# One bank for the modulation rows of eight column groups, and a new layout and order at the beginning of attention

## The chip, the cores and the metric

One core of one Trainium2 chip runs the whole program. Times are microseconds (us) on the device, from one launch to its end. A kernel is judged by the median of several runs; the profile comes from one execution and gives every instruction on the engines PE (TensorE), DVE (VectorE), ACT (ScalarE), POOL (GpSimd) and SP (SyncE, which here only issues transfers).

## The reference, cut to what matters

Two layers work on 1024 latent rows and 256 context rows of width 1024. Each begins with an adaLN modulation, whose rows come from a condition `c` for the latents and `c_ctx` for the context. Layer 0 is the attention layer and layer 1 the state-space (SSD) layer; the change lies in layer 0 and in the modulation of both.

```python
mod = silu(cond) @ w_ada[i] + b_ada[i]        # cond: c or c_ctx; 1024 x 3072 per layer
shift, scale, gate = split(mod, 3)
u = rms_normalize(h) * (1 + scale) + shift
q, k, v, g = split(u @ w_in)                  # 16 query heads of 64, 4 key/value heads
q, k = axial_rope(q), axial_rope(k)           # latents only
# latents, block of 128 queries: three neighbouring key blocks inside a band, and the 256 context keys
# context: its 256 queries see the 256 context keys
p = softmax(concat(q @ k.T / 8 (masked), sink))[..., :-1]
y = ((p @ v) * silu(g)) @ w_out
h = h + gate * y
```

## The kernel before

All matmuls of float32 data are done as three products of split operands (high and low part, `mm3`: lines L227, L228, L229), so each projection of 128 columns against 512 tokens is 24 matmuls, and against the 256 context tokens 24 shorter ones. Token groups are numbered 0 (first 512 latents), 1 (the other 512) and 2 (the context).

The kernel is written in a framework that keeps a priority per instruction (its place in the program, unless `high_priority(offset)` shifts it), orders each engine's queue from these and from the dependencies, and puts in the waits. Queues are then in order: an instruction that waits holds all behind it on its engine. `tc.issue_after(ins)` adds only an order, on the engine of `ins`. Pools are stacked in memory in the order in which they are opened; a tile of a new pool waits for those old tiles whose bytes it takes over, so what a tile lies on decides when it can first be written.

**Projection phase** (`qkvg`). After keys and values come eight column tiles of queries (`q_step`, weights `wq`) for groups 2 and 0, then eight of gates (`g_step`, `wg`) for group 2, the last four for group 0 too. A query tile passes through rope (L501 to L504 on DVE and POOL), is split (L522, L523 or L525, L526) and goes to DRAM in four transfers (L534, L535); a gate tile takes a tanh on ACT (L541), one DVE operation (L542) and one transfer (L543). Between them `fill` runs two or three steps of the list `ada`, the modulation of eight groups of 512 columns: (layer 0, n = 4, 5) and (layer 1, n = 0 to 5). A group has nine steps in `adaln_col`: eight loads of 256 KB (L181, buffers of the tags `wh` and `wl` in the pool `wv`); after every fourth load four matmuls (L185), each in its own 32 rows of the bank `aps`; and `fin`: ACT copies the bank (L189), and `modulation` turns the row with four small matmuls against `sel` (L201, two output columns), which also adds up the four row groups, and DVE adds the bias (L203). This turning is done eight times here and four times in the first phase (`ada0`).

**Attention** (`attention`). A unit is one key/value head `j` with one block `b` of 128 queries. `att_front` loads queries (`qs`, `qz` on POOL's queue, L614 and L620) and gates (`sgt`, L616), and for four heads does two-part scores into the bank pair `S` (L636 for latent keys, L637 for context keys), a masked reduction on DVE (L640) and an exponential on ACT (L642). `att_back` transposes the weights per key block (`pt`, L661), splits them (L665 on ACT, L666 on DVE), multiplies by the values (`pv`, L667 and L668), and ends with a normalisation (L674 to L684). The front runs one unit ahead (`AHEAD`). Units come in the order context (8 units of 2 key blocks), group 0 (16 units), group 1 (16 units). After each key block `tick` advances filler work in parts of three matmuls (`PARTS` = 8 for a projection): during context units the first `QC` = 5 items of the list `pr`, during group 0 the other eleven, during group 1 the output projections. `pr` holds the eight query tiles and then the eight gate tiles of group 1. A filler item first loads its weights (L220 on SP's queue), splits them (L213 on ACT, L215 on POOL), and has one bank, `pj`, for its sum.

**What lies on what.** The projection phase's pools are `wv` (17 KB a partition, with `cs32`), `wq` (30 KB: raw weights `wr`, split weights `wh`, `wl`) and `qp` (`cos`, `sin`, `qf`, `qh`, `ql`, ...). Attention's are `att` (41.5 KB, first `qz`, `qs`, then the rest), `wo` (the filler's `wr`, `wh`, `wl`) and `qp1` (`cos`, `sin`, ...). By these sizes `qz` and `qs` lie on `wv`, which the modulation uses to its end; the filler's `wr` lies on `wl` of the last gate tile, and the new `cos` on `qf`, which the last gate tile's transfer reads. In PSUM the first tile of `psT` is `S`, four banks that were `pt` and two of the four `pj`.

Of the kernel before, what the change touches and what calls it, by code (L numbers as in the profile page):

```python
# [9 lines left out]
F32 = mybir.dt.float32  # L10
# [42 lines left out]
QC = 5  # L53
TAILP = (3, 7)
# [49 lines left out]
class Kernel:  # L104
# [52 lines left out]
    def load_cond(self, p):  # L157
# [9 lines left out]
        self.sel = t(cp, [P, 2], F32, "sel")  # L167
        nc.vector.tensor_reduce(self.sel, self.ident.rearrange("p (j r) -> p r j", r=32)[:, 0:2], axis=mybir.AxisListType.X, op=ALU.add)
# [3 lines left out]
    def adaln_col(self, layer, n, pool, ps):  # L172

        nc, t = self.nc, self.t
        st = {}

        def step(k):
            if k == 0:
                st["ps"] = t(ps, [P, 512], F32, "aps", 2)
            raw = t(pool, [P, 4, P], F32, ("wh", "wl")[k // 4])  # L180
            nc.sync.dma_start(raw, self.a["w_ada"][layer, n, k].rearrange("p (a c) -> p a c", a=4))  # L181
            st[k] = raw
            if k % 4 == 3:
                for j in range(4):
                    nc.tensor.matmul(st["ps"][32 * j : 32 * j + 32], self.cs[:, k - 3 + j, :], st[k - 3 + j].rearrange("p a c -> p (a c)"), start=k == 3, stop=k == KT - 1)  # L185

        def fin():
            row = t(self.pq, [P, 512], F32, "qf")
            nc.scalar.copy(row, st["ps"])  # L189
            m = self.modulation(layer, n, row, ps)  # L190
            if n // 2 == 2 and layer == 0:
                nc.vector.tensor_scalar_mul(m, m, 0.5)

        return [lambda k=k: step(k) for k in range(KT)] + [fin]

    def modulation(self, layer, n, row, ps):
# [3 lines left out]
        for j in range(4):  # L200
            self.last_mod = nc.tensor.matmul(mt[:, 2 * j : 2 * j + 2], row[:, j * P : (j + 1) * P], self.sel, start=True, stop=True)  # L201
# [41 lines left out]
    def proj_g(self, out, pspool, ws, rH, rL, i, tag="pj", m=P, parts=1):  # L243
# [3 lines left out]
        ps = self.t(pspool, [P, 1024 if tag == "S" else 512], F32, tag)  # L247
# [50 lines left out]
    def layer0(self):  # L298
# [62 lines left out]
    def ada0(self, n, raw, ps):  # L361
# [3 lines left out]
        for k in range(KT):  # L365
            j = k % 4
            mm = nc.tensor.matmul(pj[32 * j : 32 * j + 32], self.cs[:, k, :], raw[k // 2][:, k % 2], start=k < 4, stop=k >= 4)
# [145 lines left out]
    def qk(self, p, pj, i, l=None):  # L513
        nc, t = self.nc, self.t
        n = TT[i][1]
        f = t(p, [P, 512], F32, "qf") if i < 2 else None
# [20 lines left out]
    def g_out(self, p, pj, x, i, tag="qf"):  # L537
        nc, t = self.nc, self.t
        n = TT[i][1]
        th = t(p, [P, 512], F32, tag)[:, :n]  # L540
# [10 lines left out]
    def qkvg(self, p, wk, wv, wvp):  # L551
# [35 lines left out]
        ada = []  # L587
        for layer, n in [(0, 4), (0, 5)] + [(1, n) for n in range(6)]:
            ada += self.adaln_col(layer, n, wvp, ps)
# [19 lines left out]
    def att_front(self, p, x, i, j, b):  # L609
        nc, t = self.nc, self.t  # L610
        ps = self.psA
        o = b * P - TT[i][0]
        qs = t(p, [P, R, P], F32R, "qs")
        nc.gpsimd.dma_start(qs, self.q_d[j][i][:, :, :, o : o + P].rearrange("e s d n -> (s d) e n"))  # L614
        sg = t(p, [P, 2, P], F32, "sgt")
# [13 lines left out]
        nm = t(p, [P, R], F32, "nm")  # L629
        sums = t(p, [P, R], F32, "sums")  # L630
        sms = []
        for r in range(R):
            S = t(ps, [P, 1024], F32, "S")
            for x, (qq, kk) in enumerate(((qs[:, r, :], self.kHH[j]), (qz[:, r, :], self.kL[j // 2]))):
                if k1 > k0:
                    nc.tensor.matmul(S[:, c0_:512], qq, kk[:, k0 * P : k1 * P], start=x == 0, stop=x == 1)  # L636
                nc.tensor.matmul(S[:, 512:768], qq, kk[:, LAT : LAT + CTX], start=x == 0, stop=x == 1)  # L637
            Sv = S[:, c0_:768]
            sm = t(p, [P, 640], F32, "sm")
# [8 lines left out]
        rs = t(p, [P, 2, 2, HD], F32, "rs", 2)  # L648
# [4 lines left out]
    def att_back(self, p, st, oH, oL, tick):  # L653
# [4 lines left out]
        for x, bb in enumerate(kb):  # L658
# [3 lines left out]
            ph = t(p, [P, R * P], F32R, "ph")  # L662
            pl = t(p, [P, R * P], F32R, "pl")
# [12 lines left out]
        co = t(p, [HD, 512], F32, "co")  # L676
        nc.scalar.copy(co, pv[HD:, :])
        ot = t(p, [P, 2, P], F32, "ot")
# [951 lines left out]
```

## Time and profile before

| | |
|---|---|
| Time, median of 3 runs | 1852.27 us (1848.69 to 1852.5) |
| The profiled execution | 1852.09 us, of which span 1850.4 us |
| PE busy | 1764.7 us, 95% of the span |
| DVE, ACT, POOL busy | 1171.9, 894.8, 803.8 us |
| Mean granted TensorE clock | 0.988 |
| Moved by DMA | 227.64 MB, 123 GB/s on average |

Busy time is a sum over an engine's instructions; where a wait ends, the view names the instruction that ended it. The queries and gates of the projection phase run from about 130 to 274 us, context units from 274 to about 345 us, the units of group 0 to about 526 us, and those of group 1 to about 720 us. The chain that ended last runs through PE for nearly all of the span.

### The profile page before, as it was taken

To read this page: it belongs to the slowest core of one execution; us is meant where nothing else is said; L and a number is where in the kernel's file an instruction comes from. 1 tells how busy PE (TensorE), PEld (TensorE's weight loads), DVE (VectorE), ACT (ScalarE), POOL (GpSimd) and SP (SyncE) were. 2 spreads that over 40 slices of the span, in tenths; PEclk is the share of its full clock that TensorE was granted. 3 is DMA by queue.
4 is the path that set the end of the run, shared out by engine and by line. 5 is a ranking of instruction groups with operands and counts; after the bars stand their busy time and mean duration, and the time that the engine had idled before them with its cause. 6 is when DMAs were issued, how large, how long until landed. Compare 5 with 4: busy or idle time off the path is not lost. (4 is left out here: it accounts for less than half of the span.)

```text
span 1850.4 us, 29176 instructions
## 1 busy us (share of the span) xinstructions
PE 1764.7 (95%) x10375; PEld 1506.2 (81%) x10375; DVE 1171.9 (63%) x2144; ACT 894.8 (48%) x1963; POOL 803.8 (43%) x1066
## 2 busy tenths in 40 slices
PE   6899998899999999989999999999999999999997
PEld 2697776788889687768889898988989898888886
DVE  4534426887777755684776757676675767766643
ACT  3812226677778765573443535344353534454422
POOL 2331107654456454202454554545455454554321
PEclk8999999999999999999999999999999999999998
DMA  8658856553355455321332333332232323455542
GB/s 313 233 135 254 250 160 150 132 124 88 95 129 131 105 147 169 127 67 43 83 74 78 81 77 78 80 89 69 77 93 65 86 72 99 150 170 166 177 137 69
DMA packets 212498, 227.64 MB, mean 123 GB/s; under 512 B 16384, under 2 KB 149632, under 8 KB 212352
## 3 DMA queue, kind: packets, MB, share of 16 engines
q1 hardware_dynamic: 178288, 207.12, 37.7%
q0 software_dynamic: 34064, 18.65, 5.6%
q8 instruction: 82, 1.34, 0.3%
q14 instruction: 64, 0.52, 0.1%
HBM read 190.88 MB, written 35.13 MB: 122 GB/s over the span
## 5 line engine op out<-in xcount | busy, mean ns | idle before, releaser
L227 PE MATMUL pj<-uH,wh 128*128 128x512 f32 (+1 forms) x712 | 257.7, 363 | 18.4 <-ACT uH L446 8.5
L228 PE MATMUL pj<-uL,wh 128*128 128x512 f32 (+1 forms) x712 | 244.9, 344 | 0.2 <-DVE uL L447 0.2
L229 PE MATMUL pj<-uH,wl 128*128 128x512 f32 (+1 forms) x712 | 244.2, 344 | 0.7 <-POOL wl L215 0.5
L1140 POOL TENSOR_TENSOR xw<-xn,dtdec 128x256 f32<-128x256 f32 x144 | 106.3, 741 | 197.2 <-PE psD L1165 125.0
L227 PEld LDWEIGHTS pj<-uH,wh 128*128 128x128 f32 x712 | 136.4, 192 | 48.1 <-issue 10.3
L1071 PE MATMUL pj<-uH,wh 128*128 128x512 f32 x512 | 165.6, 399 | 4.4 <-ACT bn L1025 2.4
L1071 PE MATMUL pj<-uL,wh 128*128 128x512 f32 x512 | 167.8, 401 | 1.1 <-DVE uL L291 1.1
L1071 PE MATMUL pj<-uH,wl 128*128 128x512 f32 x512 | 167.2, 401 | 0.7 <-DVE wl L1002 0.7
L215 POOL TENSOR_TENSOR wl<-wr,wh 128x512 fp32r<-128x512 f32 x92 | 123.0, 1341 | 88.3 <-ACT wh L213 87.8
L666 DVE TENSOR_TENSOR pl<-pt,ph 128x512 fp32r<-128x512 f32 x168 | 114.4, 687 | 66.3 <-ACT ph L665 65.5
L1096 PE MATMUL pj<-wh,uH 128*128 128x256 f32 x512 | 151.0, 295 | 2.6 <-ACT xn L1025 2.6
L228 PEld LDWEIGHTS pj<-uL,wh 128*128 128x128 f32 x712 | 137.0, 192 | 15.9 <-DVE uL L447 2.5
L229 PEld LDWEIGHTS pj<-uH,wl 128*128 128x128 f32 x712 | 135.9, 191 | 17.1 <-POOL wl L215 2.0
L1096 PE MATMUL pj<-wh,uL 128*128 128x256 f32 x512 | 149.1, 291 | 0.0
L1096 PE MATMUL pj<-wl,uH 128*128 128x256 f32 x512 | 146.4, 286 | 0.0
L213 ACT CAST wh<-wr 128x512 fp32r<-128x512 f32 (+1 forms) x132 | 84.7, 645 | 115.7 <-PE pj L228 83.2
L640 DVE CUSTOM_DVE_ANT_0 sm<-S,mask,nsink 128x640 f32<-128x640 f32 (+2 forms) x160 | 119.2, 771 | 21.4 <-PE S L637 13.6
L665 ACT CAST ph<-pt 128x512 fp32r<-128x512 f32 x168 | 97.4, 585 | 58.9 <-PE pt L661 55.3
L642 ACT ACTIVATE sm<-sm,nm 128x640 f32<-128x640 f32 (+2 forms) x160 | 118.7, 742 | 12.4 <-DVE nm L640 12.0
L1071 PEld LDWEIGHTS pj<-uH,wh 128*128 128x128 f32 x512 | 94.7, 189 | 25.0 <-ACT bn L1025 2.6
L1071 PEld LDWEIGHTS pj<-uL,wh 128*128 128x128 f32 x512 | 96.6, 189 | 21.9 <-DVE uL L291 2.0
L1071 PEld LDWEIGHTS pj<-uH,wl 128*128 128x128 f32 x512 | 96.4, 189 | 20.5 <-DVE wl L1002 1.1
(370 smaller groups left out, 4821.8 us busy)
## 6 DMA issues: line engine op xcount, KB each, us to landing
wr<-w_x SPq DMA_DIRECT2D x32, 512.0 KB, 5.2
M<-acs SPq DMA_DIRECT2D x64, 256.0 KB, 5.1
bw<-acs SPq DMA_DIRECT2D x64, 256.0 KB, 5.0
wr<-wo SPq DMA_DIRECT2D x48, 256.0 KB, 2.7
wr<-w_sk SPq DMA_DIRECT2D x24, 512.0 KB, 4.5
wr<-wg SPq DMA_DIRECT2D x40, 256.0 KB, 3.7
qs<-q POOLq DMA_DIRECT2D x40, 256.0 KB, 3.8
wada<-w_ada SPq DMA_DIRECT2D x16, 512.0 KB, 7.4
```

The costliest lines, as they stand in the source:

```text
L213: nc.scalar.copy(h, raw)
L215: (eng or nc.vector).tensor_tensor(l, raw, h, op=ALU.subtract)
L227: self.nc.tensor.matmul(ps, lh, rh, start=first and i == 0, stop=False)
L228: self.nc.tensor.matmul(ps, lh, rl, start=False, stop=False)
L229: self.nc.tensor.matmul(ps, ll, rh, start=False, stop=last and i == n - 1)
L640: nc.vector.tensor_tensor_reduce(out=sm[:, :W], in0=Sv, in1=self.mask[:, m0 : m0 + W], scale=-SCALE, scalar=self.nsink[:, 4 * j + r : 4 * ...
L642: nc.scalar.activation(sm[:, :W], sm[:, :W], AF.Exp, bias=nm[:, r : r + 1], scale=-1.0, accum_out=sums[:, r : r + 1])
L665: nc.scalar.copy(ph, ptf)
L666: nc.vector.tensor_sub(pl, ptf, ph)
L1071: nc.tensor.matmul(raw[:, 512 * i : 512 * i + 512], l[:, k, :], r[i][:, k, :], start=k + y == 0, stop=k == KT - 1 and y == 2)
L1096: nc.tensor.matmul(pj[:, c], l, r[:, k, :], start=c % 2 + q + k + y == 0, stop=c % 2 == 1 and q == 1 and k == 3 and y == 2)
L1140: nc.gpsimd.tensor_tensor(xw, X(st, c).rearrange("p (r h) -> p r h", r=R), self.dtdec[:, c, hd(d, g)].unsqueeze(2).broadcast_to([P, R, HP] ...
```

## The change

1. **One bank, one turning.** `ada1` replaces `adaln_col`. The eight groups accumulate in one bank: `cs46` holds the two condition columns at columns 14 and 15 among zeros, and group x takes the window of 32 columns that begins at 14 - 2x, so its two results land in rows 2x and 2x + 1 of each 32 and the other rows get zeros added. The loads and the 64 matmuls stay (the four of a set in reversed order). One `fin` remains: one copy, four small matmuls with 16 output columns, two additions and two corrections. The list `ada` has 65 steps instead of 72, so the 64 loads are spread over fewer fills.
2. **Pools by release.** `qf` and the rest of `qp` become two pools, `cs46` moves into `qp`, and attention opens `wo` first, then `back` (what `att_back` writes, and `sgt`), `sm`, `att` (with a `pad` tile of 1.5 KB ahead) and `qp1`. The filler's raw and split weights then lie on `wv`, and `qz`, `qs` on the end of `cs46` and on `cos`, `sin`.
3. **Scores in own banks.** `S` gets a pool of its own, `psS`, opened after `psT`.
4. **Early filler.** Right after the front of the first unit five parts of the first filler item are advanced (`FIRST`), in PE's order behind the last score matmul of that unit. They count towards the number that `tick` is to have done.
5. **Gates fill context units.** `pr` holds the gate tiles first, then the query tiles: context units get five gates, group 0 three gates and eight queries.

The core of the diff (`tile pool` arguments changed in the same way in `qk`, `g_out`, `att_back` are left out):

```diff
-        self.sel = t(cp, [P, 2], F32, "sel")
+        self.sel = t(cp, [P, 16], F32, "sel")
...
+    def ada1(self, pool, ps):
         nc, t = self.nc, self.t
+        order = [(0, 4), (0, 5)] + [(1, n) for n in range(6)]
+        raws = {}
+        aps = t(ps, [P, 512], F32, "aps", 2)
+        def step(s):
+            x, k = divmod(s, KT)
+            layer, n = order[x]
+            raws[s] = t(pool, [P, 512], F32, ("wh", "wl")[k // 4])
+            nc.sync.dma_start(raws[s], self.a["w_ada"][layer, n, k])
             if k % 4 == 3:
-                for j in range(4):
-                    nc.tensor.matmul(st["ps"][32 * j : 32 * j + 32], self.cs[:, k - 3 + j, :], st[k - 3 + j].rearrange("p a c -> p (a c)"), start=k == 3, stop=k == KT - 1)
+                for j in reversed(range(4)):
+                    nc.tensor.matmul(aps[32 * j : 32 * j + 32], self.cs[:, k - 3 + j, 14 - 2 * x : 46 - 2 * x], raws.pop(s - 3 + j), start=x == 0 and k == 3, stop=x == 7 and k == KT - 1)
         def fin():
             row = t(self.pq, [P, 512], F32, "qf")
-            nc.scalar.copy(row, st["ps"])
-            m = self.modulation(layer, n, row, ps)
-            if n // 2 == 2 and layer == 0:
-                nc.vector.tensor_scalar_mul(m, m, 0.5)
-        return [lambda k=k: step(k) for k in range(KT)] + [fin]
+            nc.scalar.copy(row, aps)
+            mt = t(ps, [P, 512], F32, "pt")
+            for j in range(4):
+                nc.tensor.matmul(mt[:, 16 * j : 16 * j + 16], row[:, j * P : (j + 1) * P], self.sel, start=True, stop=True)
+            v = mt[:, :64].rearrange("p (j n c) -> p n j c", n=8, c=2)
+            for layer, n0, i0, i1 in ((0, 4, 0, 2), (1, 0, 2, 8)):
+                ...
+            nc.vector.tensor_scalar_mul(self.mod[0][:, 16:], self.mod[0][:, 16:], 0.5)
+            nc.vector.tensor_scalar_add(self.mod[1][:, 8:16], self.mod[1][:, 8:16], 1.0)
+        return [lambda s=s: step(s) for s in range(8 * KT)] + [fin]
...
-        self.cs = t(wvp, [P, KT, 32], F32, "cs32")
+        self.wp = self.pool("wq", ctx=cw)
+        self.pq = self.pool("qf", ctx=cw)
+        p = self.pool("qp", ctx=cw)
+        self.cs = t(p, [P, KT, 46], F32, "cs46")
         nc.vector.memset(self.cs, 0.0)
-        nc.vector.tensor_copy(self.cs[:, :, 0:2], self.csf)
-        self.wp = self.pool("wq", ctx=cw)
-        p = self.pq = self.pool("qp", ctx=cw)
+        nc.vector.tensor_copy(self.cs[:, :, 14:16], self.csf)
...
             self.psA = self.pool("psT", space=PSUM, ctx=c1)
+            self.psS = self.pool("psS", space=PSUM, ctx=c1)
...
-            S = t(ps, [P, 1024], F32, "S")
+            S = t(self.psS, [P, 1024], F32, "S")
...
-                nc.tensor.matmul(S[:, 512:768], qq, kk[:, LAT : LAT + CTX], start=x == 0, stop=x == 1)
+                self.scored = nc.tensor.matmul(S[:, 512:768], qq, kk[:, LAT : LAT + CTX], start=x == 0, stop=x == 1)
...
-        p = self.pool("att", ctx=c0)
         BUFS.update(wr=2, wh=3, wl=3, sqt=2)
         self.wp = self.pool("wo", ctx=c0)
+        self.pb = self.pool("back", ctx=c0)
+        self.psm = self.pool("sm", ctx=c0)
+        p = self.pool("att", ctx=c0)
+        t(p, [P, 384], F32, "pad")
...
-        pr = [lambda x=x: qg1("wq", self.q_out, x) for x in range(8)] + [lambda x=x: qg1("wg", self.g_out, x) for x in range(8)]
+        pr = [lambda x=x: qg1("wg", self.g_out, x) for x in range(8)] + [lambda x=x: qg1("wq", self.q_out, x) for x in range(8)]
...
         pend = [self.att_front(p, x, *units[x]) for x in range(AHEAD)]
+        for _ in range(FIRST):
+            advance(2, self.scored.ins)
```

`advance(i, after)` is the former body of `tick`'s loop, with the instruction behind which it is queued as an argument.

More of the change, by code (lines that the diff above doesn't have):

```diff
@@ L53 @@
 QC = 5
+FIRST = 5
 TAILP = (3, 7)
@@ L200, in modulation @@
         for j in range(4):
-            self.last_mod = nc.tensor.matmul(mt[:, 2 * j : 2 * j + 2], row[:, j * P : (j + 1) * P], self.sel, start=True, stop=True)
+            self.last_mod = nc.tensor.matmul(mt[:, 2 * j : 2 * j + 2], row[:, j * P : (j + 1) * P], self.sel[:, :2], start=True, stop=True)
         m = self.mod[layer][:, n * 4 : n * 4 + 4, :]
@@ L586, in qkvg @@
                 kproj(1, i)
-        ada = []
-        for layer, n in [(0, 4), (0, 5)] + [(1, n) for n in range(6)]:
-            ada += self.adaln_col(layer, n, wvp, ps)
+        ada = self.ada1(wvp, ps)
         def fill(m):
```

68 lines of the change are left out of this document (32 added, 36 removed).

## The prediction

> **What bounds the kernel now.** I read the page first, then the busy time by stretches of the program, then the waits of PE inside the stretches that the change touches, and last the timelines of single engines there.
>
> ```profile
> span 1850.4 us, 29176 instructions
> PE 1764.7 (95%) x10375; PEld 1506.2 (81%) x10375; DVE 1171.9 (63%) x2144; ACT 894.8 (48%) x1963; POOL 803.8 (43%) x1066
> ```
>
> PE is busy for 1764.7 of 1850.4 us. What the change can win is therefore either work taken from PE, or one of the idle spots that make up the other 85.7 us. The table by stretches shows which of the two each stage has to offer (columns: stretch, its length, busy time of PE, PEld, DVE, ACT and POOL with instruction counts, granted clock, DMA share, GB/s).
>
> ```profile
> core 0: us, PE busy (x) PEld busy (x) DVE busy (x) ACT busy (x) POOL busy (x), PEclk, DMA share, GB/s
> 130.00:225.00 95.00, 95.00 (x594) 74.98 (x593) 39.46 (x78) 23.32 (x44) 15.79 (x15) 1.00 0.82 250
> 225.00:274.10 49.10, 49.10 (x309) 39.14 (x308) 12.07 (x26) 10.79 (x21) 2.81 (x4) 1.00 0.60 182
> 274.10:300.00 25.90, 19.03 (x92) 14.83 (x91) 13.74 (x46) 14.15 (x43) 14.54 (x23) 0.87 0.68 146
> 300.00:345.00 45.00, 41.19 (x220) 33.26 (x219) 35.54 (x89) 27.87 (x78) 34.68 (x47) 1.00 0.65 151
> ```
>
> From 130 to 274 us, the queries, gates and the modulation, PE has not one idle moment: only less PE work shortens it. From 274.1 to 300 PE idles for 25.90 - 19.03 = 6.87 us and its clock is down to 0.87; from 300 to 345, the rest of the context units, it idles for 3.81 us at full clock. The waits of 274 to 345 us say what ends these gaps (columns: instruction that waited, releaser, us in total, times, longest):
>
> ```profile
> PE pj L227 <- ACT wh L213: 4.2, 1, 4.2
> PE pj L227 <- DVE rope_b L502: 2.4, 3, 1.5
> PE S L637 <- DVE qf L542: 1.4, 1, 1.4
> PE S L637 <- DVE nm L640: 0.9, 3, 0.5
> ```
>
> One gap of 4.2 us is for the first filler's split weights, 1.4 us is for a bank of `S` that still holds the last gate tile (released by its L542), and 2.4 us are three waits of a filler for the one bank `pj` while rope reads the tile before.
>
> **The change part by part. Turnings.** Seven of the eight turnings in this phase go. Two of them in PE's timeline:
>
> ```profile
> 241.37 0.95 PE L201 MATMUL pt<-sel,qf 128*128 128x2 f32 x8
> 242.18 0.49 PE L228 MATMUL pj<-uL,wh 128*128 128x512 f32 x1
> ...
> 253.35 1.05 PE L201 MATMUL pt<-sel,qf 128*128 128x2 f32 x8
> 254.33 1.05 PE L185 MATMUL aps<-wh,cs 128*32 128x512 f32 x2
> ```
>
> From its start to the start of what follows, a turning holds PE for 0.81 us in the first case and 0.98 us in the second. I take 0.9, so 7 x 0.9 = 6.3 us (5.7 to 6.9), all of it on the path, since PE is full here. The new turning has 16 output columns instead of 2. No row shows that size. With as many weight loads and the same operands it lies near the old one, and I cost the difference at nothing (at most one turning's 0.9 us more). The seven ACT copies and the DVE additions that go as well are on engines with slack (ACT 23.32 and DVE 39.46 busy of 95 us). The 64 matmuls of L185 stay, 32 columns each as before. The longer memset of `cs46` and the wider sum for `sel` lie in the first microseconds, under the first weight loads: nothing, or a tenth of a microsecond.
>
> The loads lose a cover. 72 steps become 65 with the same two or three per fill, so each fill carries 9/8 of the loads. Over the eight query tiles that is 44 loads instead of 39. In the stretch 130 to 225 the bytes go from 250 x 95 = 23.75 MB to about 25.1 MB, and PE's time from 95 to about 90.6 us (some five of the seven turnings lie there). That asks for 277 GB/s and a DMA share of 0.82 x 277/250 = 0.91. It fits, with little left. What it costs PE lies between nothing and, if 250 GB/s were the most, 25.1/0.250 - 90.6 = 9.8 us. I take 0.5 us, near the lower end, because PE did not wait once at 0.82 and the next stretch has a share of only 0.60 to catch up in.
>
> **The beginning of attention.** This is PE around the last gate matmul and the first units, with the idle time ahead of a row in brackets:
>
> ```profile
> 273.94 0.39 PE L229 MATMUL pj<-uH,wl 128*128 128x512 f32 x1
> 274.17 0.28 PE L637 MATMUL S<-kHH,qs 128*128 128x256 f32 x1
> 275.80 0.39 PE L637 MATMUL S<-kHH,qs 128*128 128x256 f32 x1 [1.35 <-DVE qf L542]
> 276.02 0.40 PE L637 MATMUL S<-kL,qz 128*128 128x256 f32 x2
> ...
> 280.51 0.40 PE L667 MATMUL pv<-ph,v 128*128 128x512 f32 x1
> ...
> 285.73 0.80 PE L227 MATMUL pj<-uH,wh 128*128 128x512 f32 x1 [4.16 <-ACT wh L213]
> 286.32 0.63 PE L228 MATMUL pj<-uL,wh 128*128 128x512 f32 x1
> 286.75 0.63 PE L674 MATMUL pt<-ident,rs 128*128 128x128 f32 x2
> ...
> 289.76 0.36 PE L637 MATMUL S<-kHH,qs 128*128 128x256 f32 x1
> ...
> 292.33 0.39 PE L227 MATMUL pj<-uH,wh 128*128 128x512 f32 x1
> 292.57 0.39 PE L228 MATMUL pj<-uL,wh 128*128 128x512 f32 x1
> ```
>
> The gap of 1.35 us goes with the scores in own banks: `psS` then lies on the banks of `aps` and of two `pj` that are not the last one's. For the gap of 4.16 us the other queues tell why the weights were late:
>
> ```profile
> 275.77 0.33 SPq L543 DMA_DIRECT2D sg<-qf  x1
> 277.94 0.35 SPq L510 DMA_DIRECT2D cos<-cos  x1
> ...
> 278.81 10.56 SPq L220 DMA_DIRECT2D wr<-wq  x4
> ```
>
> ```profile
> 285.06 0.62 ACT L213 CAST wh<-wr 128x512 fp32r<-128x512 f32 x1 [4.77 <-DMA wr<-wq]
> ```
>
> On SP's queue `cos` waits for the last gate's transfer out of `qf`, on which it lies, and the filler's `wr` is issued behind it at 278.81; the data are there 6.25 us later, and ACT stood 4.77 us at the cast with the exponentials of the next unit behind it. In the new layout `wr`, `wh` and `wl` lie on `wv`, whose last user is a modulation load some ten microseconds before the last gate matmul, and `cos` on tiles that the query tiles are done with. Nothing then keeps SP from issuing the loads while the gates run, or ACT and POOL from splitting them. The early filler is 5 x 3 matmuls. A pair of rows at full clock, 292.33 and 292.57, gives 0.24 us each, so 3.6 us of work stand behind the first scores, where the chain from the first score (274.17) to the first value product (280.51) takes 6.34 us and two units of scores and the first transposes filled less than half of it.
>
> Some of it is given back. Five parts done early are what the first two ticks ask for (40 parts over 16 key blocks: 3, then 5), so the first unit's second half has no filler beside it. Its two key blocks each need the two conversions of this kind:
>
> ```profile
> 279.72 0.57 ACT L665 CAST ph<-pt 128x512 fp32r<-128x512 f32 x1
> ```
>
> ```profile
> 280.32 0.69 DVE L666 TENSOR_TENSOR pl<-pt,ph 128x512 fp32r<-128x512 f32 x1
> ```
>
> That is 2 x 1.26 = 2.5 us, with about 1 us of the next unit's scores to lie over it: 1.5 us of new idle time (0 to 2.5). So of the idle time 1.35 + 4.16 - 1.5 = 4.0 us go.
>
> With the long gap goes the slow clock behind it. From 286.32 to 286.75 a matmul takes 0.43 us instead of 0.24, and this lasts from 285.73 to about 289.76, 4.0 us at about half speed, which is 2.0 us lost. Behind the gap of 1.35 us nothing slows down. The Trainium skill, TensorE: Matmul & The Clock Gate, Part 1, has the clock halve after about 3.4 us of idle time and come back after as long a stretch of work; by that the loss would be an estimated 1.7 us and the sum below 0.3 us higher. The trace agrees on when it happens and shows a slightly longer slow stretch. The new gaps stay under the 4.16 us that brought it on, so I take all 2.0. The beginning of attention gives 4.0 + 2.0 = 6.0 us, with bounds of -1 (the stall comes back in another place) and 8.5.
>
> **Gates in the context units.** A gate tile frees `pj` after a tanh and one DVE operation, a query tile after two DVE operations, and it goes on to load DVE, POOL and SP. The 2.4 us of waits for rope go from the context units; I count 2.0. The five query tiles appear among the units of group 0, where the waits of PE from 345 to 526 us are these alone:
>
> ```profile
> PE pv L667 <- ACT ph L665: 2.9, 4, 1.4
> PE pv L668 <- DVE pl L666: 1.7, 3, 1.2
> ```
>
> Three query tiles lay there already and none made PE wait for rope, since 88 parts over 76 key blocks come at about one part a block and leave time between two tiles. I cost the five more at 0.3 us in all (0 if like those three, 5 x 0.8 = 4.0 if like the three waits in the context units). The last filler of group 0 is now a query tile: its rope chain and four transfers stand before the first weight loads of the output projection on SP's queue, which has idle time there to take them; nothing, at most 1 us.
>
> **The sum.** 6.3 - 0.5 + 6.0 + 2.0 - 0.3 = 13.5 us. The profiled execution took 1852.1 us (span 1850.4 and 1.7 around it), which is within 0.2 us of the median of 1852.27. The forecast is 1852.1 - 13.5 = 1838.6 us. All later stages keep their instructions and should move up as they are.
>
> **The rivals.** *The weights still come late.* SP's order may leave the `wr` loads behind the last gate transfer (275.77). With the same 6.25 us to ACT's cast the first filler could start at about 282.7, and PE would stand from the end of the scores, about 276.4, for 6.3 us instead of 5.5, in front of the first transposes and with the slow clock again. The beginning of attention then loses 0.8 us instead of winning 6.0: 1845.4 us. For it speaks that SP is in order and full of gate transfers; against it that nothing the loads need is late any more. Chance 0.15.
>
> *The projection phase is bound by its transfers once PE has less to do.* By the bounds above, 250 GB/s as the most would take the whole win of the turnings: 6.3 - 0.5 = 5.8 us less, 1844.4 us. For it speaks the share of 0.82. Beside it stands a rule of the Trainium skill, Perfetto Trace Analysis, What "DMA-bound" means: an issuing queue that is solid with transfers is a bound of its own, whatever the data rate. Against it speaks that PE never waited. Chance 0.12.
>
> *Rope hurts among the units of group 0.* At the mean of the three waits in the context units, 0.8 us, all eight query tiles there cost 6.4 us: 1838.6 + 6.1 = 1844.7 us. DVE is the busiest helper there, but the three tiles of before waited for nothing. Chance 0.07.
>
> *Slower: the modulation loads come behind PE.* The place is the query tiles, where a set of four loads needs buffers that the set before frees, and the reversed order frees the first buffer last. One set of before, its issue, the landing time of its kind, and the matmuls that use it:
>
> ```profile
> 215.64 1.98 SPq L181 DMA_DIRECT2D wh<-w_ada  x4
> ```
>
> ```profile
> wh<-w_ada SPq DMA_DIRECT2D x32, 256.0 KB, 4.4
> ```
>
> ```profile
> 223.35 1.06 PE L185 MATMUL aps<-wh,cs 128*32 128x512 f32 x8
> ```
>
> The four are issued by 217.6 and land by about 222.0, so the lead is 1.3 us. There are 16 sets, and PE is in order: each late set stops everything. The whole gain of 13.5 us is gone when a set is late by 0.84 us on average; at 1.2 us it is 19.2 us, 1857.8 us. Against it: all sets would have to lose their lead, and the gate tiles leave the queue time. Chance 0.07.
>
> *It does not do what it says.* If the queues come out with the gaps where they were and the loads cost what the turnings win, the time is 1849 to 1853 us. Chance 0.05.
>
> **How the numbers follow.** The forecast has 0.54, with a range of its own of 1833 to 1843 us: the bounds of the beginning of attention (8.5) and of the turnings (6.9) on the one side, 4 us of the unknown costs on the other. The three rivals at 1844 to 1846 have 0.34 together. A range of 1831 to 1847 us holds these cases and leaves out the last two and the outer tails, about 0.18. A measurement of this kernel can tell about 0.2%, 3.7 us, from no change. Faster than that: 0.54 + 0.15 + 0.12 + 0.07 = 0.88. Within it: 0.05. Slower: 0.07.
>
> **What would show it.** In the profile after, L201 has 4 matmuls behind the projections instead of 32, and PE is still full up to the first score, which comes about 6 us earlier. The wait of L227 for L213 and that of `S` for L542 are gone, L220's first loads of the filler lie ahead of the last gate transfer, and the granted clock stays at 1.00 through the first units. In the context units the wait for `rope_b` is gone, and it does not appear among the units of group 0. I am wrong in the sum if L185 waits for a load, if a gap over 3 us stays ahead of the first filler, or if L227 waits for L502 after 345 us.

## The result and the profile after

The changed kernel took 1838.4 us (median of 6 runs, 1831.21 to 1842.44) against 1851.88 us before (1847.52 to 1855.22): a ratio of 0.9934, interval 0.9916 to 0.9952. The forecast was 1838.6 us, in a range of 1831 to 1847. The total is right; the terms below it are not all right, and that is what the experiments are about.

The head of the page after:

```profile
span 1839.2 us, 29059 instructions
PE 1757.5 (96%) x10319; PEld 1503.1 (82%) x10319; DVE 1171.9 (64%) x2136; ACT 893.0 (49%) x1956; POOL 803.2 (44%) x1066
```

The span is 11.2 us shorter and PE is busy for 7.2 us less; the 56 matmul records fewer are the seven turnings. PE's idle time, span minus busy, is 81.7 us against 85.7. These two totals mix gains and losses of different stages, and busy time also grows when the clock is low, so they don't tell the parts apart. Nor does the chain that ended last: on the page before, its shares of the span add up to about 2%, and it reaches back only to 1797 us. That PE bounds the projections rests on its busy time there. The stretches, with the columns of the prediction's table, cut now at the new first score (267 to 268 us):

```profile
core 0: us, PE busy (x) PEld busy (x) DVE busy (x) ACT busy (x) POOL busy (x), PEclk, DMA share, GB/s
130.00:225.00 95.00, 95.00 (x598) 74.89 (x597) 40.22 (x75) 22.15 (x43) 16.70 (x16) 1.00 0.86 270
225.00:267.00 42.00, 41.32 (x259) 33.66 (x258) 12.21 (x21) 10.61 (x21) 6.62 (x7) 1.00 0.73 221
267.00:300.00 33.00, 29.94 (x158) 24.16 (x158) 18.72 (x60) 20.82 (x60) 17.79 (x29) 1.00 0.47 113
300.00:345.00 45.00, 43.29 (x259) 36.84 (x258) 32.71 (x92) 33.46 (x90) 29.90 (x51) 1.00 0.56 129
```

PE is still full to 225 us, at a DMA share of 0.86 instead of 0.82. After that it is idle once, for 0.68 us, and the beginning of attention idles for 3.06 us up to 300 us, at a clock of 1.00, where it had 6.87 us at 0.87. The waits of PE from 100 to 267 us, from 267 to 300 and from 300 to 345:

```profile
PE aps L188 <- DMA wl<-w_ada: 0.7, 1, 0.7
...
PE S L646 <- DVE qz L711: 1.8, 1, 1.8
PE S L646 <- DVE nm L649: 1.1, 2, 0.6
...
PE pv L676 <- ACT ph L674: 1.4, 2, 0.9
```

The waits for split weights (4.2 us), for the last gate tile's bank (1.4) and for `rope_b` (2.4) are gone. One is new: 1.8 us for the zeroing of `qz`. PE's timeline at the beginning of attention:

```profile
250.60 0.96 PE L195 MATMUL pt<-sel,qf 128*128 128x16 f32 x8
...
268.41 0.40 PE L238 MATMUL pj<-uH,wl 128*128 128x512 f32 x1
268.64 0.40 PE L646 MATMUL S<-kHH,qs 128*128 128x256 f32 x2
...
270.86 0.50 PE L646 MATMUL S<-kL,qz 128*128 128x256 f32 x2 [1.82 <-DVE qz L711]
...
273.28 0.39 PE L236 MATMUL pj<-uH,wh 128*128 128x512 f32 x1
```

The one turning left is done at 250.60. The first score begins at 268.64 instead of 274.17, the first filler at 273.28 instead of 285.73.

**Where the time went, by stage.** I cut each trace at PE entries that every kernel has: the 450th projection matmul of the program, the last gate matmul, the value product that ends the context units, those that end group 0 (92nd run of value products), the next 18 (the crossing into group 1), the 168th (end of attention), and the first `psD` matmul of the next layer. Each stage's length is the difference of two starts in one execution.

| kernel | start | projections | context | group 0 | crossing | group 1 | to `psD` | rest | span |
|---|---|---|---|---|---|---|---|---|---|
| before | 130.4 | 143.5 | 75.8 | 178.9 | 37.8 | 155.9 | 55.0 | 1073.1 | 1850.4 |
| before again | 130.2 | 143.5 | 75.5 | 178.9 | 37.8 | 156.1 | 54.5 | 1073.7 | 1850.2 |
| changed | 132.5 | 135.9 | 63.1 | 180.5 | 41.1 | 156.1 | 60.2 | 1069.8 | 1839.2 |
| changed again | 126.8 | 136.7 | 64.9 | 180.5 | 41.2 | 155.5 | 60.4 | 1072.2 | 1838.3 |
| turning only | 125.8 | 138.0 | 72.1 | 179.6 | 37.8 | 155.2 | 54.3 | 1069.7 | 1832.4 |
| turning only, again | 129.7 | 135.6 | 72.9 | 179.4 | 37.8 | 155.2 | 54.6 | 1073.8 | 1839.0 |
| no early filler | 128.6 | 136.4 | 65.3 | 181.0 | 41.3 | 155.5 | 60.2 | 1072.3 | 1840.6 |
| queries first | 129.7 | 135.7 | 71.3 | 180.4 | 38.1 | 155.6 | 60.0 | 1069.3 | 1840.1 |
| pools as before | 129.7 | 134.6 | 69.3 | 178.6 | 42.5 | 155.4 | 58.2 | 1069.5 | 1837.9 |
| `S` in `psT` | 124.8 | 136.1 | 64.7 | 180.6 | 42.7 | 155.9 | 56.7 | 1069.8 | 1831.1 |
| gates last | 127.6 | 135.8 | 63.3 | 179.3 | 38.1 | 155.3 | 63.5 | 1071.0 | 1834.0 |
| three edits | 124.6 | 136.2 | 65.0 | 179.4 | 38.1 | 155.7 | 57.4 | 1070.6 | 1827.0 |
| three edits, again | 127.6 | 136.6 | 64.7 | 179.2 | 38.1 | 155.6 | 58.9 | 1073.0 | 1833.7 |
| turning and order | 129.0 | 134.9 | 66.6 | 178.2 | 37.8 | 155.3 | 54.8 | 1071.4 | 1828.0 |

Two executions of one kernel differ by up to 5.7 us at the start and 4.1 us in the rest, by up to 2.4 us in the projections, and by at most 1.8 us in each of the stages between. So start and rest tell nothing here, and the middle columns carry the reading. From before to changed: projections -7.6 us, context units -12.7, group 0 +1.6, crossing +3.3, the way to `psD` +5.2. Two gains are larger than forecast, and two stages that were costed at about nothing lose 8.5 us together.

A stage's length also holds the granted clock in that one execution, which no edit sets directly. Over the context units it is 1.00 in the changed kernel's first execution and in the run with gates last; 0.97 in the repetition, without early filler, with `S` in `psT`, in both runs of the three edits and with turning and order; and 0.95 in the other six. On the way to `psD` it lies between 0.92 and 1.00. A share of 0.03 lost over 60 us is 1.8 us at the most, and less where PE idles anyway, so differences of this size are read together with the clock.

### The profile page after: what moved, and what is told of

It is laid out like the page before. It is cut to its first block, busy times and chain, and to the rows that moved or that the text cites. A ratio compares the mean times of both kernels' runs of the same rounds, so it can differ in the third digit from the quotient of the medians.

```text
span 1839.2 us, 29059 instructions
## 1 busy us (share of the span) xinstructions
PE 1757.5 (96%) x10319; PEld 1503.1 (82%) x10319; DVE 1171.9 (64%) x2136; ACT 893.0 (49%) x1956; POOL 803.2 (44%) x1066
## 3 DMA queue, kind: packets, MB, share of 16 engines
q1 hardware_dynamic: 178288, 207.12, 37.8%
## 5 line engine op out<-in xcount | busy, mean ns | idle before, releaser
L236 PEld LDWEIGHTS pj<-uH,wh 128*128 128x128 f32 x712 | 135.8, 191 | 39.2 <-ACT uH L457 9.6
L675 DVE TENSOR_TENSOR pl<-pt,ph 128x512 fp32r<-128x512 f32 x168 | 114.5, 687 | 58.2 <-ACT ph L674 57.0
L237 PEld LDWEIGHTS pj<-uL,wh 128*128 128x128 f32 x712 | 136.0, 191 | 16.9 <-issue 3.1
```

The costliest lines, as they stand in the source:

```text
L236: self.nc.tensor.matmul(ps, lh, rh, start=first and i == 0, stop=False)
L237: self.nc.tensor.matmul(ps, lh, rl, start=False, stop=False)
L675: nc.vector.tensor_sub(pl, ptf, ph)
```

## The experiments

Each undoes or adds one part, or a few. Times are medians, ratios stand against the kernel before on the same chip, with their intervals.

**The turning alone.** Before, with `ada1`, `cs46` (in `wv`) and the 16 columns of `sel` only; run twice, on two chips.

```diff
...
-        ada = []
-        for layer, n in [(0, 4), (0, 5)] + [(1, n) for n in range(6)]:
-            ada += self.adaln_col(layer, n, wvp, ps)
+        ada = self.ada1(wvp, ps)
```

> The kernel before with the first part alone: one bank, one turning, 65 steps; pools, scores' banks, filler and order as before. Theory (turnings are PE work on a full PE): the first score comes at 268 to 269 us instead of 274.2, the context units from the first score to the 16th value product take 75.6 us as before, and the total is 5 to 6 us under the kernel before, about 1846. Rival (the denser loads take it back, and all of the gain was attention's): the first score stays at 273 to 275 us, L185's successor waits for loads several times, and the total is within 1 us of before.

> The kernel before with one bank and one turning alone, timed again beside the others of this call. Theory (the turnings win 6 to 8 us, the stall ahead of the first filler shrinks as well since the loads of the first units come earlier): context units 72 us, total 1838 us, 12 us under before. Rival (1836.7 came from favourable first loads): total 1842 to 1844.

1836.71 us, 0.9919 (0.9897 to 0.994), and again 1838.68 us, 0.9943 (0.9921 to 0.9965). The first expectation, about 1846 us with context units as before, missed. Both lie inside the whole change's interval: in the total, the other four parts add nothing that can be told. By stage the turning gives 5.5 and 7.9 us in the projections (PE waits 1.9 and 1.0 us there for a modulation load), and 3.2 us in the context units as well (72.5 against 75.7, means of two). Its waits from 255 to 345 us show what is left there:

```profile
PE pj L235 <- DVE rope_b L510: 2.8, 2, 2.4
PE S L643 <- DVE qf L550: 1.3, 1, 1.3
```

The bank and the rope waits are as before, but the 4.2 us for the split weights are gone without any new pools. In this trace SP issues `cos` 0.52 us behind the last gate's transfer (265.67 and 266.19) where it took 2.17 us before, and the filler's first cast starts 4.2 us behind the first of its loads (267.08 to 271.26) where it took 6.25. I put the first of these down to another rotation of the `qf` buffers, but no run tests it.

**No early filler.**

```diff
-FIRST = 5
+FIRST = 0
```

> The changed kernel with FIRST = 0: no parts ahead of the first tick, the rest as changed. Theory (the early parts cover the first softmax chain, and the layout makes them possible): PE idles 3 to 4 us more between the first scores and the first transposes, 1 to 1.5 us of it comes back because the first two ticks now have their five parts, so the stretch from the first score to the 16th value product is 65 to 66 us instead of 62.9, total 2 to 3 us over the changed kernel. Rival (the layout does it alone): that stretch stays at 62 to 64 us and the total within 1 us.

1839.66 us, 0.9933 (0.991 to 0.9957). The context units take 65.3 us, as expected, against 63.1 and 64.9: 1.3 us on the mean, within what two executions differ. One wait of 1.5 us is new there, of a score for `pl` (L646 for L675), but against the repetition, which has the same clock of 0.97, the stage is only 0.4 us longer. No effect on the time is shown.

**Queries first again**, the rest as changed.

```diff
-        pr = [... "wg" ...] + [... "wq" ...]
+        pr = [... "wq" ...] + [... "wg" ...]
```

> The changed kernel with the old order of the filler items, queries first. Theory (the order wins in the context units and loses later): the context stretch is 65.5 to 68 us instead of 62.9 with the waits for rope back, the units of group 0 (16th to 92nd value product) take 179 us instead of 180.5 and the crossing to group 1 (92nd to 110th) 38 instead of 41.1; the total is within 2 us of the changed kernel. Rival (as predicted: 2.0 won in the context units, 0.3 lost later): total 1.7 us over the changed kernel, and the crossing stays at 41 us, since it has another cause.

1840.43 us, 0.9931 (0.9906 to 0.9957). The crossing came out as expected; the context units (65.5 to 68) and group 0 (179) had been expected shorter. The context units go back up by 7.3 us (71.3 against the mean of 64.0), and the crossing comes back from 41.2 to 38.1 us. The order does both, and in the median they nearly cancel. The waits from 265.4 to 336.7 us, and the clock behind the first scores:

```profile
PE S L646 <- DVE qz L711: 1.8, 1, 1.8
PE pj L236 <- DVE rope_b L513: 1.8, 2, 1.4
```

```profile
269.40:273.40 4.00, 3.70 (x11) 2.85 (x10) 1.57 (x7) 2.01 (x9) 1.96 (x5) 0.50 0.29 56
273.40:277.40 4.00, 4.00 (x21) 3.30 (x20) 0.43 (x3) 0.62 (x1) 1.52 (x2) 0.80 0.25 43
```

1.8 us is the rope wait and about 2.8 the low clock (4.0 us at 0.50 and 4.0 at 0.80). The changed kernel's repetition has up to 1.7 us of such a loss in the same place with the order unchanged (64.9 us at 0.97), so not all of it belongs to the order. The other 2.7 us I can't put on single rows.

**Pools as before**: `cs46` on `wv`, one pool for `qf` and the rest, `att` first, then `wo`, no `pad`.

```diff
...
-        self.pb = self.pool("back", ctx=c0)
-        self.psm = self.pool("sm", ctx=c0)
-        p = self.pool("att", ctx=c0)
+        p = self.pb = self.psm = self.pool("att", ctx=c0)
...
```

> The changed kernel with the pools stacked as before (cs46 on wv, qf in qp, att first, then wo and qp1, no pad); scores in own banks, early filler and order of items stay. Theory (what the filler's weights lie on decides when they can be loaded): the first cast of the filler's weights waits for its load until about 10 us after the last gate matmul, PE stands 5 to 7 us in front of the first filler and its clock falls below 0.9 there; the context stretch is 69 to 72 us instead of 62.9, total 6 to 9 us over the changed kernel. Rival (asking for the filler early is enough): the stretch is at most 65 us.

1838.05 us, 0.9925 (0.9904 to 0.9945). The context units lose 5.3 us (69.3 against 64.0), and one wait there has half of it:

```profile
PE pj L236 <- ACT wh L222: 2.6, 1, 2.6
```

The clock has part of the rest: 0.52 from 272.4 to 276.4 us and 0.63 from there to 280.4. That is what was expected of the context units. But group 0 is 1.9 us shorter and the way to `psD` 2.1 us (the clock is 1.00 there, 0.97 in the changed kernel), against 1.4 us more at the crossing (clock 0.96), and the total, expected 6 to 9 us higher, is the same. So in the median the layout gives nothing either.

**The changed kernel again, and scores in `psT`'s banks.**

```diff
-            self.psS = self.pool("psS", space=PSUM, ctx=c1)
+            self.psS = self.psA
```

> The changed kernel once more, to see how far one execution's stretches repeat. Theory (the stretches belong to the order of the queues): projections from the last key or value product to the last gate matmul, context units 62.9 us, units of group 0 180.5, crossing to group 1 41.1, and 60.2 us from the last value product to the first psD matmul come again within 1 us each; only the stretch before the first modulation loads moves by some microseconds. Rival (the differences between kernels are those of single executions): stretches move by 2 us and more. Total about 1838.

> The changed kernel with S back in the pool psT, so that it comes first in PSUM as before. Theory (the 5 us lost after attention come from the new places of the banks, which the next pools meet): from the last value product to the first psD matmul 55 to 57 us instead of 60.2, the first score's second head waits 1.3 us for the last gate tile, which hides under the 1.8 us that it waits for the zeroing of qz anyway; total 3 to 4 us under the changed kernel. Rival (the loss comes from the pools in SBUF, which decide when the SSD weights can be loaded): 60 us as in the changed kernel, total the same.

The repetition gave 1837.51 us, 0.9933 (0.9921 to 0.9945); its context units moved by 1.8 us, more than expected. `S` in `psT` gave 1837.25 us, 0.9929 (0.9915 to 0.9943), where 3 to 4 us less had been expected: context units 64.7, as changed, 1.5 us more at the crossing (42.7 against 41.2, at a clock of 0.96), and 3.6 us less on the way to `psD` (56.7 against 60.3). That stage in PE's timeline, changed first, then with `S` in `psT`:

```profile
759.61 0.80 PE L236 MATMUL pj<-uH,wdth 128*128 128x512 f32 x1 [2.83 <-ACT dt L899]
...
769.37 0.39 PE L1078 MATMUL psD<-uH,wh 128*128 128x256 f32 x1 [1.74 <-ACT sqa L369]
```

```profile
755.08 0.50 PE L236 MATMUL pj<-uH,wdth 128*128 128x512 f32 x1 [1.57 <-ACT dt L899]
...
761.25 0.68 PE L1078 MATMUL psD<-uH,wh 128*128 128x256 f32 x1
```

With own banks the first `psD` matmul waits 1.74 us for an ACT copy out of a bank that it takes over. Five of the six traces with own banks have this wait (the sixth, without the early filler, waits 1.1 us there for `dt`), and none of the eight others has it. The bank arrangement of attention thus sets a wait in the layer behind it. The wait of `wdth`'s projection for `dt` is 1.26 us longer here, but it doesn't follow the banks: it is 0.8 us in all six traces with the old pools, one of them with own banks, and anything from 0.8 to 2.8 us in the eight with the new ones.

**Gates at both ends**: five gates in the context units, then the queries, then the last three gates.

```diff
+        gate, query = (...)
+        pr = gate[:QC] + query + gate[QC:]
```

> The changed kernel with the filler items in the order five gates, eight queries, three gates. Theory (the 3.3 us lost at the crossing to group 1 are the rope and split of the last query tile in DVE's queue, in front of the units' own work): context units 62.9 us as in the changed kernel, crossing 37.5 to 38.5 us instead of 41.1, total 3 us under the changed kernel. Rival (the crossing is lost to the weights of the output projection, which take over the place of the last items): crossing stays at 41 us.

1835.82 us, 0.9922 (0.991 to 0.9935). Context 63.3, as changed; crossing 38.1, as before. So the 3.3 us at the crossing come from a query tile being the last filler of group 0. DVE's and PE's timelines of the changed kernel show how:

```profile
515.88 1.23 DVE L534 TENSOR_TENSOR ql<-qf,qh 128x512 fp32r<-128x512 f32 x1
517.03 1.27 DVE L675 TENSOR_TENSOR pl<-pt,ph 128x512 fp32r<-128x512 f32 x2
```

```profile
517.76 0.50 PE L677 MATMUL pv<-pl,v 128*128 128x512 f32 x1 [1.40 <-DVE pl L675]
```

The split of the last query tile stands in DVE's queue ahead of the unit's own `pl`, and PE stands 1.40 us for that. But the way to `psD` is 63.5 us here, 3.2 us more than changed. The clock has most of this. These are the ways to `psD` of the changed kernel, with gates last, with pools as before, and of the kernel with turning and order that comes below:

```profile
709.17:769.37 60.20, 51.91 (x221) 38.77 (x221) 33.74 (x47) 30.16 (x53) 19.92 (x16) 0.97 0.58 186
```

```profile
699.46:763.00 63.54, 54.05 (x222) 40.65 (x221) 33.69 (x47) 30.11 (x53) 19.77 (x16) 0.92 0.55 176
```

```profile
710.23:768.44 58.21, 50.95 (x222) 37.60 (x221) 34.00 (x47) 30.17 (x53) 20.51 (x16) 1.00 0.58 192
```

```profile
701.87:756.64 54.77, 50.22 (x221) 37.61 (x221) 34.20 (x45) 28.03 (x48) 20.07 (x16) 1.00 0.61 204
```

At 0.92 instead of 0.97 some 3 us more are lost to the clock (0.08 x 63.5 against 0.03 x 60.2). Why it falls lower with gates last is not settled.

**Three edits**: the two before together, and the zeroing of `qz` on POOL; run twice, on two chips.

```diff
-            nc.vector.memset(self.qz[z][...].bitcast(F32), 0.0)
+            nc.gpsimd.memset(self.qz[z][...].bitcast(F32), 0.0)
```

> The changed kernel with three edits: S in psT, gates last in the list, and qz zeroed on POOL instead of DVE. Theory (each loss has the cause given to it): crossing 38 us, from the last value product to the first psD matmul 55 to 57, the wait of 1.8 us for qz gone and 1.3 us for the last gate tile in its place; total 6 to 7 us under the changed kernel, about 1831 to 1832. Rival (a saved wait comes back in the next stage): total within 2 us of the changed kernel.

> The changed kernel with S in psT, gates last in the list and qz zeroed on POOL, timed again beside the others of this call. Theory: 1832 us, 5 to 6 us under the changed kernel and 4 to 5 us under one turning alone. Rival: within 2 us of one turning alone.

1831.73 us, 0.9909 (0.9893 to 0.9926), and 1834.32 us, 0.9914 (0.9891 to 0.9937). The first run is as expected, the second 2.6 us slower, and 4.4 us under the turning alone on the same chip. The crossing (38.1) and the way to `psD` (57.4, 58.9, both at a clock of 0.94) keep both repairs. The context units (65.0, 64.7) are no shorter than with `qz` zeroed on DVE. In both runs the 1.8 us for `qz` are gone, the last gate tile's bank has 1.3 us instead, and two waits for DVE's reduction have grown from 1.1 to 1.6 us:

```profile
PE S L646 <- DVE nm L649: 1.6, 2, 1.1
PE S L646 <- DVE qf L553: 1.3, 1, 1.3
```

**Before again, and before with the turning and the order only**: pools, banks of `S` and beginning of attention as before, `pr` as in the run with gates at both ends.

> The kernel before once more, to see how far its one execution's stretches repeat. Theory: projections (450th projection matmul to the last gate matmul) 143.5 us, context units 75.8, units of group 0 178.9, crossing 37.8, group 1 155.9, last value product to first psD matmul 55.0, each within 1 to 2 us; the stretch before the 450th projection matmul, 130.4 us, moves by some microseconds, and the SSD layer's 1073 us may come out at 1070 as in the other kernels. Rival: the context units, whose stall hangs on when a transfer lands, move by more than 3 us.

> The kernel before with one turning and the filler order five gates, eight queries, three gates; pools, S and early filler as before. Theory (in the context units order, pools and early filler each remove part of the same idle time): context units 66 to 69 us, crossing 38, last value product to first psD matmul 54 to 55 since S and pools lie as before; total 4 to 5 us under the kernel with one turning alone and within 2 us of the one with three edits. Rival (the order is worth nothing while the first weights are late): context units 71 to 72 us.

Before again: 1852.17 us, 1.0012 (0.999 to 1.0035), which is the size of a difference that means nothing. Turning and order: 1829.33 us, 0.9896 (0.9873 to 0.9919), the fastest of all by the median; its interval ends below that of the changed kernel's repetition and overlaps the first one's by 0.0003. The total was expected 4 to 5 us under the kernel with the turning alone; on the same chip it is 9.35 under it. The order alone takes the context units from 72.5 to 66.6 us (the clock from 0.95 to 0.97), as expected, and no later stage loses anything. Its page, its context units as one stretch, and PE on the way to `psD`:

```profile
span 1828.0 us, 29052 instructions
```

```profile
263.90:330.50 66.60, 62.80 (x335) 51.48 (x335) 41.91 (x128) 46.92 (x133) 45.48 (x71) 0.97 0.62 158
```

```profile
750.48 0.50 PE L235 MATMUL pj<-uH,wdth 128*128 128x512 f32 x1 [0.78 <-ACT dt L889]
756.64 0.68 PE L1068 MATMUL psD<-uH,wh 128*128 128x256 f32 x1
```

The same two rows of the kernel before:

```profile
771.25 0.51 PE L227 MATMUL pj<-uH,wdth 128*128 128x512 f32 x1 [0.78 <-ACT dt L882]
777.33 0.68 PE L1061 MATMUL psD<-uH,wh 128*128 128x256 f32 x1
```

With the old banks and pools neither wait of the changed kernel is there: 0.78 us for `dt`, as before, and none at `psD`. The 1.3 us for the last gate tile's bank, which the old banks keep, is less than the 1.74 us that the new ones cost at `psD` alone.

## Why the prediction was right, and where it was not

**Turnings: right in size, with one effect overlooked.** Forecast 6.3 - 0.5 = 5.8 us. The two kernels before take 143.5 us in the projections, the twelve traces with one turning 136.0 on the mean (134.6 to 138.0): 7.5 us. In the trace before, six of the eight turnings hold PE for 0.81 us and two for 0.98, so the seven that went are worth 6.0 us, 0.86 each. The two longer ones stand inside a set of modulation matmuls and split it. This is the second of them:

```profile
252.36 1.06 PE L185 MATMUL aps<-wh,cs 128*32 128x512 f32 x6
253.35 1.05 PE L201 MATMUL pt<-sel,qf 128*128 128x2 f32 x8
254.33 1.05 PE L185 MATMUL aps<-wh,cs 128*32 128x512 f32 x2
255.31 0.39 PE L227 MATMUL pj<-uH,wh 128*128 128x256 f32 x1
```

A whole set (x8) holds PE for 1.0 us. The split one holds it for 0.99 us ahead of the turning and for 0.98 us again behind it, so each of the two splits costs about another 1.0 us, 1.9 together. The prediction shows the last part of the set (x2) and counts all of L185 as work that stays. In the changed kernel all sixteen sets run whole. 6.0 + 1.9 - 0.7 of waiting is 7.2 of the first execution's 7.6 us. The 16 columns cost nothing (0.96 us for the row, 0.95 for 2 columns). The loads' lost cover cost 0.68 us in one wait, 0.5 forecast. The prediction named a wait of the modulation matmuls for a load as a sign that its sum is wrong; it came in eleven of the twelve traces, 0.4 to 1.9 us long.

**Beginning of attention and gates: right in kind, too small, and wrongly divided.** Forecast 6.0 + 2.0 = 8.0 us; the context units became 11.7 us shorter (75.7 to 64.0, means of two). The waits to go went. The granted clock of 1.00, which the sum counted on for 2.0 us, came in the first execution but not in the repetition, and in only one of the ten other traces with one turning; that it came there is luck. Over the context units as a whole PE's idle time fell from 10.8 to 3.5 us:

```profile
274.10:349.70 75.60, 64.78 (x332) 51.58 (x331) 53.22 (x146) 45.92 (x129) 53.20 (x74) 0.95 0.66 149
```

```profile
268.60:331.40 62.80, 59.29 (x331) 49.41 (x330) 42.41 (x130) 44.60 (x127) 41.53 (x68) 1.00 0.58 137
```

Between these two rows 7.3 us are idle time and 5.5 us are busy time of nearly the same number of matmuls. The low clock has about 2.0 of the 5.5, by the prediction's own reading of 285.73 to 289.76 us; the other 3.5 I did not trace, and no term of the sum stood for them. The mis-sized term is the gates in the context units. I counted 2.0 us, the rope waits alone. Put back, the order costs 7.3 us; done alone on the turning, it gives 5.9. Both figures hold some 2 us of low clock. The prediction gave the 4.2 us for split weights to the new pools, but in the run of the turning alone they go too. The early filler, whose 3.6 us of cover I counted, has no shown effect. What is lost when single parts are taken out (7.3, 5.3, 1.3 and at most 0.7 for own banks) adds up to 14.6 us, but together they give only 8.5 beyond the turning's 72.5. So a part taken out costs more than its share of the gain: without the order or without the pools the clock falls to 0.95 as well. Such losses can't be added up as gains.

**"Nothing, at most 1 us": failed.** I looked at SP's queue for what the last query tile of group 0 delays. What delays the crossing is a query tile as the last filler of group 0: it cost 3.3 us, as the order's three variants show. 1.40 us of this stand in the row above, behind DVE's queue. The rival of rope among the units of group 0 had the engine right, but it did not come as a wait for `rope_b`: the units' own `pl` stood behind the rope. Inside group 0 the loss is 1.6 us (0.3 forecast). PE's waits there, from 331.5 to 512 us, are these:

```profile
PE pv L677 <- DVE pl L675: 2.8, 7, 0.7
PE pv L676 <- ACT ph L674: 1.5, 2, 0.9
```

They have moved from ACT's `ph` to DVE's `pl`, but their sum of 4.3 us is no more than the 4.6 before (2.9 and 1.7). So the 1.6 us lie in PE's busy time, 176.0 us instead of 174.3. Its cause stays open: with the old pools group 0 takes 178.6 us, and with queries first 180.4, of which up to 1.8 are the clock (0.99 instead of 1.00).

**"All later stages ... should move up as they are": failed.** The way to `psD` lost 5.6 us on the means of two (60.3 against 54.75). The clock has up to 1.8 of it (0.97 in both executions, 1.00 before). The own banks of `S` have most of the rest: the two traces with old pools that are shown above at a clock of 1.00 take 58.2 us with own banks and 54.8 without, though they differ in the early filler and the order too. One wait of 1.74 us at `psD` is the banks' for sure. Whether the new pools cost anything of their own is not shown; the wait for `dt`, up to 2.8 us with them and 0.8 without, speaks for it. I had asked only what `S` waits for in its new banks, not what takes over these banks afterwards.

**The new wait.** The prediction expected up to 2.5 us of new idle time behind the first unit. That did not come: from 267 to 300 us PE waits only for `qz` and the reductions. What came is 1.82 us inside the first unit's scores: in DVE's queue the zeroing of `qz` stands behind the last gate's operation.

```profile
269.47 0.69 DVE L553 SCALAR_TENSOR_TENSOR qf<-qf,pj 128x512 f32<-128x512 f32 x1 [5.27 <-ACT qf L552]
270.32 0.48 DVE L711 MEMSET qz<- 64x512 f32 x1 [0.16 <-issue]
```

**The rivals.** The weights did not come late: SP issues the first filler's loads far ahead of the last gate matmul (268.41) and the last gate's transfer.

```profile
246.82 7.62 SPq L229 DMA_DIRECT2D wr<-wg  x4
...
270.19 0.33 SPq L554 DMA_DIRECT2D sg<-qf  x1
```

The projections are not bound by transfers: 270 GB/s passed, above the 250 that this rival took as the most, with 0.68 us of waiting. The modulation loads fell behind by this wait alone.

In sum, 5.8 + 8.0 - 0.3 = 13.5 was forecast. Against the means of two, the stages from the projections to `psD` gave 7.2 + 11.7 - 1.6 - 3.3 - 5.6 + 0.2 = 8.6 us; start and rest add 3.0, less than two executions of one kernel differ by there, and the medians of six runs differ by 13.5. So a right total came of gains forecast too small and losses left out, which is luck. By the medians the turning alone gives as much as the whole change.

## What to carry to other kernels

An edit that shifts work between stages is read stage by stage, against two executions of the same code: here the medians of the changed kernel and four of its variants lay within 3.2 us of each other, while single stages differed by up to 8 us, in both directions. The granted clock of each stage is read beside its length. When a tile gets other banks or bytes, ask who takes these over next as well as who held them before. Work put in as filler is placed by what stands behind it on the helper's in-order queue at the end of its stage, not by whether PE has room for it; and what single parts cost when they are taken out is not added up as their gain.

## What the runs showed of the hardware

The prediction held that gaps of PE under 4.16 us leave the clock at full speed. They don't always. In the repetition of the changed kernel, with no gap over 1.82 us, the clock fell to 0.63 behind 4 us in which PE was busy for 1.65:

```profile
263.50:267.50 4.00, 1.65 (x8) 0.97 (x6) 1.98 (x6) 1.12 (x3) 0.00 (x0) 1.00 0.17 66
267.50:271.50 4.00, 3.46 (x10) 2.78 (x11) 1.56 (x7) 1.98 (x8) 2.17 (x5) 0.63 0.41 77
```

In the first execution the same instructions ran through the same sparse spot at full clock, and so they did with gates last, behind 4.00 us with 1.64 us of work:

```profile
268.40:273.20 4.80, 1.91 (x10) 1.23 (x9) 2.79 (x8) 1.48 (x4) 0.00 (x0) 1.00 0.14 55
273.20:276.00 2.80, 2.80 (x14) 2.33 (x14) 0.76 (x5) 1.61 (x7) 1.80 (x4) 1.00 0.35 67
```

The two executions' context units differ by 1.8 us, which fits a loss of 4 us x 0.37 = 1.5. The Trainium skill, TensorE: Matmul & The Clock Gate, Part 1, has a free-running window of about 3.4 us, by which the moment of the switch varies from run to run. The traces agree that it varies. That a stretch without a gap of that length can bring the slow clock too is shown by the first two rows above.
